# Moving the cross-attention's value products to the front of a streaming-encoder block, and seven more weight pairs by seven products

## The chip, the cores and the metric

The kernel runs on one core of a Trainium2 chip. A core has five engines with queues of their own: TensorE (PE, matmuls; its weight loads are shown as PEld), VectorE (DVE), ScalarE (ACT), GpSimd (POOL, which here issues transfers and a few memsets) and SyncE (SP, which issues most transfers). Operands lie in an on-chip memory of 128 partitions (SBUF); matmuls write to eight banks of a second memory (PSUM), from which VectorE or ScalarE take the results. The metric is the device time of one execution in microseconds; the figure given is the median of several.

## The reference

One layer of an encoder block on 256 positions of width 2048, all in float32, with 256 memory tokens:

```python
x = x + 0.5 * swiglu(rms_norm(x, ffn1_norm), ffn1_w_up, ffn1_w_down)      # d_ff = 5632
h = rms_norm(x, mix_norm);  proj = h @ w_in                              # 10240 columns
...                                  # gated recurrence, convolution with RG-LRU, gated merge
x = x + merged @ w_out
x = x + cross_attention(rms_norm(x, xattn_norm), rms_norm(mem, mem_norm), wq, wkv, wo)
x = x + 0.5 * swiglu(rms_norm(x, ffn2_norm), ffn2_w_up, ffn2_w_down)
return rms_norm(x, final_norm)

def cross_attention(h, m, wq, wkv, wo):                                  # 4 heads of 512
    q = (h @ wq).reshape(B, S, 4, 512)
    k, v = jnp.split(m @ wkv, 2, axis=-1)                                # from mem alone
    p = softmax(einsum('bshd,bmhd->bhsm', q, k) * 512 ** -0.5)
    return einsum('bhsm,bmhd->bshd', p, v).reshape(B, S, D) @ wo
```

The keys and the values depend on the memory tokens and their weights only, not on x.

## The kernel before, in words

**Arithmetic.** Every large product is made from operands split in two parts: a high part, rounded to the format that TensorE multiplies (`h`), and the rest (`l`). A product is then three matmuls: high by high, low by high, high by low (`three`, L905; `rows_product`, L696). ACT writes the high part and DVE subtracts it from the raw weight to get the low one (`split`, L532).

**Weights.** All weights are read from DRAM in pieces of 1 MB, 128 x 2048 numbers each, in a list that is drawn up beforehand (`plan`, L541 on) and followed two pieces ahead (`weights`, L585). A piece is made ready in one of four ways (`prepare`, L636): "plain" is a load and one split of 2048 columns; "added" (`begin_added`, L627) lets ACT write the negative high part and a transfer issued by POOL add the raw weight to it, so that DVE has nothing to do; "fast" adds four sums of weight blocks (two of them in one instruction) and splits 1536 columns of the weight and 2048 of the sums; "made" reads such sums from DRAM, where they were put earlier.

**Feed-forwards.** The up weights of a feed-forward are 11 groups of 8 pairs (g, p). A pair is two row blocks by two column blocks, for two halves of the 256 positions. Eight block products of three matmuls each (24 matmuls of 512 columns) give the plain result; a Strassen-like scheme does it with seven products (21 matmuls) by means of sums of the blocks of x and of the weights (`PRODUCTS`, L917). "mixed" is eight products that add into the same seven PSUM banks as "fast" pairs. Which pair goes which way is in `MIXED` (L43) and `ffn_order` (L50). Before, in the first feed-forward, group 0 is "plain" throughout, groups 1 and 2 have four mixed pairs (0, 2, 4, 6) and four fast ones, the later groups one mixed pair (6, "added") and seven fast ones. The down products (24 matmuls a piece) follow some groups behind. The operands of x are made at the start (`head_x`, L1044; `operand_pairs`, L860): h and l for each pair, the blocks' sums, and the differences that mixed pairs need (`less`).

**The middle.** 176 products of 24 matmuls' time each, with recurrences beside them: input projection, gates, branches, out, then the cross-attention: 16 query products, 16 key products, 16 value products (`wvm`), 16 of `wo`. During the queries the memory tokens are loaded, normalised and split (`ms`, eight of the 24 smaller tiles), and their squares are summed; one fp32 product makes the scale of each token along the columns, and two small ones make it by token. The scores of the four heads (`scores`, L1465) are put among the value products, one step behind each (`pump`). Beside the middle's products POOL loads 56 pieces of the second feed-forward's up weights, DVE makes their sums, and POOL writes these to DRAM (`make_ahead`, L604; `make_sums`, L612): 56 in 154 products.

**Memory.** Tiles of 128 x 2048 ("big": raw, td, h, l, tl, made, own, ev, junk) come from one ring of 9, which has 4 more in the feed-forwards (`FFN_POOLS`, L789). Tiles of 128 x 1024 ("slot") are 24.

**Order.** The program is recorded as operations (`Flow.record`, L211), then put in order by a planner (`arrange`, L291): each operation gets a price (`price`, L254) and a due time, worked back from the matmuls that need it (`aims`, L282), and a list scheduler fills the five queues. It gives out tiles and PSUM banks as they come free by its own prices, and runs twice; the second time with the waits for reused tiles that the first gave. Every queue then runs in that fixed order, so nearly all instructions show the recorder's line, L465.

Of the kernel before, what the change touches and what calls it, by code (L numbers as in the profile page):

```python
# [14 lines left out]
P = 128  # L15
T = 256
# [14 lines left out]
for _name, _n in [  # L31
# [12 lines left out]
    "ffn1": {0: "plain", 1: (0, 2, 4, 6), 3: (6,)},  # L44
    "ffn2": {0: "fast", 1: (), 3: ()},
# [3 lines left out]

def ffn_order(name):  # L50
    mixed = MIXED[name]
    out, down = [(mixed[0], 0, p) for p in range(8)], [("down", 0, 1, c, 0) for c in range(4)]
    for g in range(1, NG):
        if g < 3:
            out += [("mixed" if p in mixed[1] else "fast", g, p) for p in (0, 1, 2, 3, 5, 4, 7, 6)]
        else:
            out += [("mixed" if p in mixed[3] else "fast", g, p) for p in (1, 3, 0, 6, 4, 2, 5, 7)]
# [38 lines left out]
class Buffer(View):  # L96


    def __init__(self, ring, shape, dt, name, room, whole=False):
        grain = shape[1] if whole else 1 if shape[1] <= 128 else 32  # L100
        super().__init__(self, np.arange(shape[1]) // grain)
        self.ring, self.shape, self.dt, self.name, self.room = ring, shape, dt, name, room
# [7 lines left out]
class Ring:  # L110
    def __init__(self, tag, spare):
        self.tag, self.spare = tag, spare
        self.places, self.takers = [], []
# [70 lines left out]
class Flow:  # L184
# [26 lines left out]
    def record(self, queue, method, args, kw):  # L211
# [16 lines left out]
        for v in outs:  # L228
            t = v.tile
            if not t.users:  # L230
                op.takes.append(t)
                t.ring.takers.append(op)
            elif t.users[-1].queue is queue and t.users[-1] is not op:
                op.deps.setdefault(t.users[-1], False)
# [56 lines left out]
    def arrange(self):  # L291
# [178 lines left out]
def block_kernel(tc: tile.TileContext, xT, xin, memT, vec, gfin, bgate, lruw, wu1, wd1, win, wv,  # L470
# [72 lines left out]
    def plan_ffn(name, wu, wd):  # L543
        for e in orders[name]:
            src = wd[e[4], e[3]] if e[0] == "down" else wu[e[1], e[2]]
# [30 lines left out]
    for name, w in (("mv", wvm), ("o", wo)):  # L576
        for g in range(4):
            plan_rows(name, w, g)
    between = between + 2, len(plan) - between - 6
    plan_ffn("ffn2", wu2, wd2)  # L580

    head, rest = [], {}
    planned = count()

    def weights(*key):  # L585
        while plan and len(ahead) < 2:
# [3 lines left out]
            if i < len(head):  # L590
# [13 lines left out]
    def make_ahead(i):  # L604
        n, pieces = len(MADE), between[1] - 16
# [183 lines left out]
    FFN_POOLS = dict(more=4, third=1)  # L789
# [70 lines left out]
    def operand_pairs(name, src, gain, q, xg, out):  # L860
        mixed = MIXED[name]
        both = [p for p in mixed[1] if p not in mixed[3]]

        for a in src:
# [7 lines left out]
            less = None if 2 * q + i not in mixed[1] else (h[:, 512:768], l[:, 512:768])  # L872
            if 2 * q + i in both:
                if 2 * q + i == both[0]:
                    xd.append(slot(F32R, "xd"))
                n = 512 * both.index(2 * q + i)
                less = [xd[-1][:, a:a + 256] for a in (n, n + 256)] if n < 1024 else []
            out.append(((h, l), less))

        def sums(which=((0, "less"), (0, "sums"), (1, "less"), (1, "sums"))):  # L880
            s = slot(name="xs")
            for i, ((h, l), less) in enumerate(out):
# [8 lines left out]
                if less == [] and (i, "less") in which:  # L891
                    third = scoped["third"].tile([P, 512], F32R, name="xd", tag="xd")
                    less.extend((third[:, :256], third[:, 256:]))
                if less and (i, "less") in which:
                    made(*less, 2, 0, lambda o: ((a[0], a[1], ALU.subtract), (a[2], a[3], ALU.subtract)))
                if 2 * q + i not in mixed[3] and (i, "sums") in which:
                    if not i and less and len(which) > 1:
                        s = slot(name="xs")
# [14 lines left out]
    def part(pair, i, n):  # L913
# [7 lines left out]
        "plain": [(0, 0, 1), (1, 0, 2), (0, 1, 0), (1, 1, 3), (2, 2, 1), (3, 2, 2), (2, 3, 0), (3, 3, 3)],  # L921
    }

    def ffn(name, pairs, sq, then, begin=(), sums=(), rstds=()):
# [5 lines left out]
        for e in order:  # L930
            if e[0] != "down":
# [40 lines left out]
        for at, e in enumerate(order):  # L972
# [3 lines left out]
            if kind != "down":  # L976
# [13 lines left out]
                last = at + 1 == len(order) or order[at + 1][1] != g or following == "down"  # L990
                ends = kind != "plain" and uses[g, 0][-1][0] == p
                if ends or last:
                    if ends or kind == "plain":
                        flow.room = room["scope"]
                        ev = big("ev", F32)
                        e0, e1, e2, e3 = (ev[:, i * 512:(i + 1) * 512] for i in range(4))
                        if rstds:
                            rstd = rstds[0]
                        if rstd is None:
                            rstd = sq.rstd_tokens()  # L1000
                if ends:
# [3 lines left out]
                if last:  # L1005
                    if kind == "plain":
                        activate(e0, accs[0], accs[1], 0)
                        activate(e3, accs[3], accs[2], 1)
                    else:
                        for o, n, x in ((e0, 1, e0), (e1, 3, e1), (e1, 2, e1)):  # L1010
                            dve.tensor_tensor(out=o, in0=accs[n], in1=x, op=ALU.add)
                        activate(e0, e0, e1, 0)
                        for o, n, x in ((e3, 6, e2), (e2, 3, e2)):
                            dve.tensor_tensor(out=o, in0=accs[n], in1=x, op=ALU.add)
                        activate(e3, e3, e2, 1)
# [48 lines left out]
    head += [lambda p=p: head_x(p) for p in range(8)]  # L1064
# [6 lines left out]
    for i in range(3):  # L1071
        rest[4 + i] = lambda i=i: head_residual(i)
    for q, i in enumerate((3, 7, 8, 9)):
        rest[i] = lambda q=q: sums1[q](((0, "less"), (1, "sums")))
    made = rest[7], rest[8]
    rest[7] = lambda: [f() for f in (lambda: head_residual(3), made[0])]
    rest[8] = lambda: [f() for f in (head_rstd, made[1])]
    for q, i in ((0, 22), (1, 23), (2, 24)):
        rest[i] = lambda q=q: sums1[q](((0, "sums"),))
# [37 lines left out]
    def to_mix(c, t):  # L1117
# [9 lines left out]
        else:  # L1127
            late2.append(lambda: normed(xs2, c, "mix_norm"))

# [312 lines left out]
    ms, sqm = Operands(), Squares()  # L1442
    for m in range(KT):
# [5 lines left out]
        for i in range(2 * m, 2 * m + 2) if m < 4 else (m + 4,) if m < 12 else ():  # L1449
# [5 lines left out]
            sqm.add(mk)  # L1455
    ks = Operands()
    for m in range(KT):
        acc = product(ms.tiles, weights("k", m))
        if m == 0:
            rmem, rmtok = sqm.rstd(), sqm.rstd_tokens()  # L1460
        ks.add(summed(acc, by=rmem))

    probs = {}
# [31 lines left out]
    side += [scores(h) for h in range(HEADS)]  # L1495
    vs = {}
    for g in range(4):
        accs = [bank(), bank()]
        for kq in range(4):
            rows_product(accs, ms.tiles, weights("mv", g, kq), 4 * kq, kq == 0, kq == 3)  # L1500
            pump(1)
        for t in range(2):
            s = slot(F32R, "vs")
            f = scoped["tmp2"].tile([P, 512], F32, name="vf", tag="part")
            act.activation(f, accs[t], ACT.Copy, scale=rmtok[:, t:t + 1])
# [155 lines left out]
```

## Time and profile before

| | |
|---|---|
| median of 3 runs | 2416.41 us (2416.34 to 2417.48) |
| the profiled execution | 2415.88 us, of it 2414.1 us between first and last instruction |
| PE busy | 2402.7 us, 12130 matmuls |
| DVE busy | 2066.0 us, 2232 instructions |
| ACT busy | 1421.3 us |
| moved by DMA | 662.83 MB, mean 275 GB/s |

The page gives the busy times and forty slices of the span of 60 us each; a digit is a share in tenths. The first feed-forward takes slices 1 to 11 or 12, the middle up to about the 29th, the second feed-forward the rest. The listings give for a group of instructions: engine, operation, what is written and read, the shapes, the count, the busy time, the mean of one in ns, and the idle time of the engine before them. A row of the timeline is start, duration, engine and instruction; a row of the chain is start, duration and what. A row of the table by stretches has the stretch, its length, then busy time and count for PE, PEld, DVE, ACT and POOL, the granted clock of PE, the share of the DMA engines and GB/s. PE's matmuls overlap, so 0.39 us for one is its latency, and the distance of two starts is what it costs.

### The profile page before, as it was taken

Reading aid. Unit: us, or ns where it says so; the run is one execution under the profiler, and the core shown is the slowest. Engines: PE = TensorE matmul, PEld = TensorE weight load, DVE = VectorE, ACT = ScalarE, POOL = GpSimd, SP = SyncE. Lnnn points to the kernel's source line nnn. Section 1 sums busy time; section 2 is a strip of 40 time slices with the busy share of each in tenths; the row PEclk is TensorE's granted clock in tenths of the full one; section 3 lists DMA queues with packets and bytes.
Section 4 is the critical chain, followed back from the end, with each engine's and each line's share of the span. In section 5 each row is a group of like instructions: output and inputs, shape, how many; then the busy total and the mean of one; then the engine's idle time right before and its main releaser. Section 6 shows DMA issues by size and latency. Waiting matters only on the chain.

```text
span 2414.1 us, 30928 instructions
## 1 busy us (share of the span) xinstructions
PE 2402.7 (100%) x12130; PEld 2011.3 (83%) x12130; DVE 2066.0 (86%) x2232; ACT 1421.3 (59%) x1414; POOL 83.2 (3%) x142
## 2 busy tenths in 40 slices
PE   9999999999999999999999999999999999999998
PEld 8888888888888888888888888888888888888887
DVE  8999999999955778788876887767899999999995
ACT  8566666666754443476534654445677666666663
POOL 0000000000000000000000000000000000000000
PEclk9999999999999999999999999999999999999999
DMA  8568787888735688888988988876898677777773
GB/s 317 192 227 261 261 261 244 261 261 258 265 140 192 236 300 296 306 310 313 367 311 315 344 324 325 314 277 253 331 393 316 254 262 261 261 261 261 261 274 114
DMA packets 98354, 662.83 MB, mean 275 GB/s; under 512 B 10912, under 2 KB 11168, under 8 KB 24992
## 3 DMA queue, kind: packets, MB, share of 16 engines
q1 hardware_dynamic: 77904, 517.11, 57.7%
q0 software_dynamic: 19584, 142.62, 18.0%
q8 instruction: 95, 1.56, 0.3%
q10 hardware_dynamic: 720, 1.13, 0.1%
q14 instruction: 51, 0.42, 0.0%
HBM read 574.83 MB, written 60.82 MB: 263 GB/s over the span
## 4 chain that ended last, share of the span: by engine, by line
PE 98%; ACT 1%; DVE 1%; DMA 1%; issue 0%; ACTq 0%; DVEq 0%
PE acc L465 98%; DMA made<-wu 1%; ACT h L465 0%; PE warm L465 0%; DVE l L465 0%; ACT ops L465 0%; DVE made L465 0%; DVE ops L465 0%; ACT junk L465 0%; ACT x L465 0%; DVE ss L465 0%; DVE x L465 0%; DVE gate L465 0%; DVE xc L465 0%; ACTq L465 0%
## 5 line engine op out<-in xcount | busy, mean ns | idle before, releaser
L465 DVE TENSOR_TENSOR l<-raw,h 128x2048 fp32r<-128x2048 f32 (+2 forms) x428 | 870.2, 2037 | 181.4 <-ACT h L465 72.3
L465 ACT ACTIVATE h<-raw 128x2048 fp32r<-128x2048 f32 (+2 forms) x428 | 730.8, 1712 | 401.0 <-PE acc L465 222.8
L465 PE MATMUL acc<-h,xh 128*128 128x512 f32 x1244 | 484.5, 390 | 0.9 <-ACT h L465 0.9
L465 PE MATMUL acc<-h,xl 128*128 128x512 f32 x1244 | 484.0, 389 | 0.0
L465 ACT ACTIVATE h<-td 128x1024 fp32r<-128x1024 f32 (+1 forms) x248 | 307.9, 1250 | 225.4 <-DVE td L465 212.8
L465 PE MATMUL acc<-h,ops 128*128 128x512 f32 x1664 | 398.0, 391 | 0.6 <-DVE gate L465 0.6
L465 DVE TENSOR_TENSOR tl<-td,h 128x1024 fp32r<-128x1024 f32 (+1 forms) x248 | 358.8, 1457 | 16.7 <-ACT h L465 14.8
L465 PEld LDWEIGHTS acc<-h,ops 128*128 128x128 f32 x1664 | 310.0, 188 | 64.8 <-DVE gate L465 1.1
L465 PE MATMUL acc<-h,hidop 128*128 128x512 f32 x1408 | 355.2, 390 | 0.0
L465 PEld LDWEIGHTS acc<-h,hidop 128*128 128x128 f32 x1408 | 262.9, 188 | 53.7
L465 PE MATMUL acc<-ops,h 128*128 128x512 f32 x1152 | 278.3, 393 | 0.3 <-DVE ops L465 0.2
L465 PEld LDWEIGHTS acc<-h,xh 128*128 128x128 f32 x1244 | 233.6, 188 | 51.2 <-ACT h L465 1.5
L465 PEld LDWEIGHTS acc<-h,xl 128*128 128x128 f32 x1244 | 233.6, 188 | 48.1
L465 PEld LDWEIGHTS acc<-ops,h 128*128 128x128 f32 x1152 | 211.6, 188 | 43.3 <-DVE ops L465 1.2
L465 PE MATMUL acc<-l,ops 128*128 128x512 f32 x832 | 206.2, 389 | 0.0
L465 PE MATMUL acc<-l,hidop 128*128 128x512 f32 x704 | 190.3, 389 | 0.0
L465 PEld LDWEIGHTS acc<-l,ops 128*128 128x128 f32 x832 | 155.9, 188 | 32.3
L465 PE MATMUL acc<-l,xh 128*128 128x512 f32 x636 | 175.9, 390 | 0.0
L465 PE MATMUL acc<-tl,xh 128*128 128x512 f32 x608 | 168.2, 390 | 0.0
L465 DVE TENSOR_TENSOR made<-made 128x512 f32<-128x512 f32 x224 | 152.9, 687 | 11.9 <-DMA made<-wu 8.0
L465 PEld LDWEIGHTS acc<-l,hidop 128*128 128x128 f32 x704 | 132.2, 188 | 27.5
L465 PEld LDWEIGHTS acc<-ops,l 128*128 128x128 f32 x1152 | 148.0, 191 | 5.6
(172 smaller groups left out, 1921.9 us busy)
## 6 DMA issues: line engine op xcount, KB each, us to landing
raw<-wu SPq DMA_DIRECT2D x108, 1024.0 KB, 7.0
raw<-wd SPq DMA_DIRECT2D x72, 1024.0 KB, 6.9
made<-wu POOLq DMA_DIRECT2D x56, 1024.0 KB, 6.6
kept<-made POOLq DMA_DIRECT2D x56, 1024.0 KB, 7.1
td<-kept SPq DMA_DIRECT2D x56, 1024.0 KB, 7.2
raw<-wu SPq DMA_DIRECT2D x56, 768.0 KB, 5.6
raw<-win SPq DMA_DIRECT2D x40, 1024.0 KB, 4.8
raw<-wg SPq DMA_DIRECT2D x32, 1024.0 KB, 6.2
```

Of the source, the lines that this page charges most:

```text
L465: getattr(op.queue.real, method)(*map(real, args), **{k: real(v) for k, v in kw.items()})
```

## The change

In the first feed-forward, groups 0, 1 and 2 now have the mixed pairs 0, 4 and 6 (6 as "added") and five fast pairs. The "plain" scheme of a group is gone, and with it a small pool of one tile. The 16 value products of the cross-attention are done in the first feed-forward: three sets of four before group 0, the fourth between groups 0 and 1. The memory tokens are loaded and split for them into four big tiles; they are loaded once more as rows, to be squared with a sum over each row for the scale. Each set's result goes through a small tile to DRAM (512 KB each, issued by POOL) and is read back and split among the key products, beside which the scores of a head now stand. The memory is loaded and split again for the keys, as before. The 56 sums are spread over 140 products of the middle, from 6 products earlier in relation to its start. In its first pass the planner now also knows that a PSUM bank must be read before it is taken again.

```diff
-    "ffn1": {0: "plain", 1: (0, 2, 4, 6), 3: (6,)},
-    "ffn2": {0: "fast", 1: (), 3: ()},
+    "ffn1": ((0, 4, 6), (0, 4, 6), (0, 4, 6)) + ((6,),) * (NG - 3),
+    "ffn2": ((),) * NG,
...
+VALUES = {0: (0, 1, 2), 1: (3,)}
...
+        if name == "ffn1":
+            out += [("mv", i, kq) for i in VALUES.get(g, ()) for kq in range(4)]
+        out += [("mixed" if p in mixed[g] else "fast", g, p)
+                for p in ((0, 4, 1, 2, 6, 3, 5, 7) if g < 3 else (1, 3, 0, 6, 4, 2, 5, 7))]
...
+        if not hasattr(self, "sequence"):
+            for r in {id(t.ring): t.ring for op in ops for t in op.takes if t.whole}.values():
+                for t, op in zip(r.tiles, r.takers[len(r.places):]):
+                    for u in t.users:
+                        if u.i < op.i:
+                            u.after.append(op)
...
-            if e[0] == "mixed" and e[1] > 2:
-                kind = "added"
+            if e[0] == "mixed":
+                kind = "added" if e[1] > 2 or e[2] == 6 else kind
...
-    between = between + 2, len(plan) - between - 6
+    between = between - 4, len(plan) - between
...
-        n, pieces = len(MADE), between[1] - 16
+        n, pieces = len(MADE), between[1] - 20
...
-    FFN_POOLS = dict(more=4, third=1)
+    FFN_POOLS = dict(more=4)
...
+    class BigOperands(Operands):
+        def new(self):
+            i = len(self.tiles) % 4
+            if i == 0:
+                flow.room = room["scope"]
+                self.cur = big("ms")
+            self.tiles.append(self.cur[:, i * 512:(i + 1) * 512])
+            return self.tiles[-1]
...
+    def head_memory(kq):
+        m = slot(name="mem")
+        n = T if kq == 0 else 4 * T
+        for a in range(0, 4 * T, n):
+            sp.dma_start(m[:, a:a + n], memT[:, 4 * kq * T + a:][:, :n])
+            for j in range(a, a + n, T):
+                ms1.add(m[:, j:j + T], col("mem_norm", 4 * kq + j // T))
+
+    def head_squares():
+        ss = small.tile([P, 2 + PAD], F32, name="ssm", tag="ssm", bufs=1)[:, :2]
+        for t in range(2):
+            m = big("memory", F32)
+            sp.dma_start(m, mem[t])
+            act.activation(m, m, ACT.Square, accum_out=ss[:, t:t + 1])
+        act.activation(ss, ss, ACT.Sqrt, bias=eps, scale=1.0 / D)
+        dve.reciprocal(out=rmtok, in_=ss)
+
+    head.update({kq: lambda kq=kq: head_memory(kq) for kq in range(4)})
...
+    def memory_values(g, kq, w):
+        if kq == 0:
+            values[g] = [bank(), bank()]
+        accs = values[g]
+        rows_product(accs, ms1.tiles, w, 4 * kq, kq == 0, kq == 3)
+        if kq == 3:
+            f = slot(name="values")
+            for t in range(2):
+                act.activation(f[:, t * 512:(t + 1) * 512], accs[t], ACT.Copy, scale=rmtok[:, t:t + 1])
+            values[g] = dram.tile([P, 1024], F32, name=f"values{g}", tag=f"values{g}")
+            gps.dma_start(values[g], f)
...
-    ms, sqm = Operands(), Squares()
+    ms = Operands()
...
+    def take_values(g):
+        f = slot(name="values")
+        sp.dma_start(f, values[g])
         for t in range(2):
             s = slot(F32R, "vs")
+            r = f[:, t * 512:(t + 1) * 512]
+            split(s[:, :512], s[:, 512:], r)
             vs[g, t] = s
+
+    for m in range(KT):
+        acc = product(ms.tiles, weights("k", m))
+        if m == 0:
+            rmem = by_feature(rmtok)
+        ks.add(summed(acc, by=rmem))
+        if m % 4 == 3:
+            side.append(scores(m // 4))
+            take_values(m // 4)
+        pump(1)
     pump(1 << 30)
```

More of the change, by code (lines that the diff above doesn't have):

```diff
@@ L467, in emit, with block_kernel @@
                 inner.close()
-def block_kernel(tc: tile.TileContext, xT, xin, memT, vec, gfin, bgate, lruw, wu1, wd1, win, wv,
+def block_kernel(tc: tile.TileContext, xT, xin, memT, mem, vec, gfin, bgate, lruw, wu1, wd1, win, wv,
                  wg, wab, wout, wq, wk, wvm, wo, wu2, wd2, out_):
@@ L889, in made @@
                     split(h, l, s[:, at:at + n * P])
[L891 to L898, printed above, removed]
+                if less:
+                    made(*less, 2, 512 * i, lambda o: ((a[0], a[1], ALU.subtract), (a[2], a[3], ALU.subtract)))
+                if 2 * q + i in both:
+                    s = slot(name="xs")
+                if 2 * q + i not in mixed[-1]:
                     made(h[:, 512:], l[:, 512:], 4, 512 * i,
@@ L1454, in block_kernel @@
             ms.add(mk, col("mem_norm", i))
[L1455 to L1463, printed above, removed]
+    probs, ks, vs = {}, Operands(), {}
     def scores(h):
```

122 lines of the change are left out of this document (54 added, 68 removed).

## The prediction

> **What bounds the kernel now.** I read the page first: the busy times, then the slices.
>
> ```profile
> span 2414.1 us, 30928 instructions
> PE 2402.7 (100%) x12130; PEld 2011.3 (83%) x12130; DVE 2066.0 (86%) x2232; ACT 1421.3 (59%) x1414; POOL 83.2 (3%) x142
> PE   9999999999999999999999999999999999999998
> DVE  8999999999955778788876887767899999999995
> DMA  8568787888735688888988988876898677777773
> ```
>
> TensorE is busy throughout, VectorE is nearly full in the two feed-forwards (the first eleven and the last nine slices) and has room in the middle. Since a busy PE isn't yet a PE at its rate, the next views were the chain of waits and the timeline of PE.
>
> ```profile
> 7.13 104.75 PE acc L465 x470
> 111.89 583.11 PE acc L465 x2618
> ```
>
> ```profile
> 304.41 0.39 PE L465 MATMUL acc<-h,xh 128*128 128x512 f32 x1
> 309.17 0.39 PE L465 MATMUL acc<-h,xh 128*128 128x512 f32 x1
> ```
>
> The chain is one string of products. The two PE rows are the first matmuls of two consecutive seven-product pairs: 21 matmuls in 4.76 us, 0.2267 us each, which is also the commonest step between neighbours everywhere else. So a saved matmul is worth 0.2267 us, and there are hardly any holes to win. The waits of PE's weight loads confirm that: the one on VectorE's last split is the third longest, six times and 1.4 us in all.
>
> ```profile
> PEld acc L465 <- ACT h L465: 1.5, 2, 1.1
> PEld acc L465 <- DVE tl L465: 1.4, 6, 0.4
> PEld acc L465 <- DVE gate L465: 1.1, 1, 1.1
> ```
>
> The shapes in the listing by form give VectorE's prices, and one of ACT's (count, then busy us and mean ns):
>
> ```profile
> L465 DVE TENSOR_TENSOR l<-raw,h 128x2048 fp32r<-128x2048 f32 x260 | 593.8, 2287 | 168.9 <-ACT h L465 66.4 <-PE acc L465 53.7 <-issue 26.4
> L465 DVE TENSOR_TENSOR l<-raw,h 128x1536 fp32r<-128x1536 f32 x152 | 266.0, 1751 | 12.0 <-ACT h L465 5.6 <-PE acc L465 5.3 <-DMA l<-own 0.3
> L465 DVE TENSOR_TENSOR tl<-td,h 128x1024 fp32r<-128x1024 f32 x192 | 232.5, 1216 | 14.7 <-ACT h L465 13.3 <-PE acc L465 1.1
> L465 DVE TENSOR_TENSOR td<-raw,td 128x512 f32<-128x512 f32 x192 | 131.0, 682 | 0.4
> L465 DVE TENSOR_TENSOR td<-raw 128x1024 f32<-128x1024 f32 x96 | 116.7, 1216 | 0.7 <-PE acc L465 0.7
> L465 DVE TENSOR_TENSOR ev<-acc,ev 128x512 f32<-128x512 f32 x147 | 97.6, 685 | 12.5 <-PE acc L465 9.5 <-ACT ev L465 1.2
> L465 DVE SCALAR_TENSOR_TENSOR ev<-ev,rtok 128x512 f32<-128x512 f32 x42 | 31.3, 745 | 0.0
> L465 DVE TENSOR_TENSOR hidop<-acc,hidop 128x512 fp32r<-128x512 f32 x44 | 28.7, 681 | 0.7 <-ACT hidop L465 0.7
> L465 DVE TENSOR_TENSOR xl<-xg,xh 128x512 fp32r<-128x512 f32 x16 | 10.8, 683 | 0.4 <-ACT xh L465 0.4
> L465 DVE TENSOR_TENSOR xs<-xg 128x128 f32<-128x128 f32 x38 | 10.6, 284 | 4.5 <-ACT xg L465 4.2
> L465 ACT ACTIVATE ops<-mem,vt 128x256 fp32r<-128x256 f32 x16 | 7.0, 501 | 0.0
> L465 DVE SCALAR_TENSOR_TENSOR ops<-mem,vt,ops 128x256 fp32r<-128x256 f32 x16 | 7.0, 478 | 0.0
> ```
>
> A pair by seven products costs VectorE 1.216 + 2 x 0.682 + 1.751 + 2 x 1.216 = 6.76 us against 4.76 us of PE; a pair by eight costs 2.29 us against 24 x 0.2267 = 5.44, and one of kind "added" nothing. That is why not every pair goes by seven.
>
> **The change, part by part.** *Seven pairs.* Group 0 goes from none by seven to five, groups 1 and 2 from four to five each: seven pairs, 3 matmuls each, 21 x 0.2267 = 4.76 us less PE. This is on the path.
>
> *The values' products.* Their 16 x 24 matmuls (87.1 us of PE) move from the cross-attention to the front, at no change for PE. Their splits move along (16 x 2.29 = 36.6 us of VectorE), so each four of them bring 21.8 us of PE for 9.2 of VectorE.
>
> *Is VectorE enough at the front?* Group 0 with its twelve value products: twelve splits 27.4, pairs 0 and 4 4.6, five by seven 33.8, pair 6 nothing, sixteen memory operands 7.6, low parts of x 5.5, sums of x 7 x (4 x 0.284 + 0.683) + 3 x about 1 = 15.7, eviction 7 x 0.685 + 2 x 0.745 = 6.3, turned hidden 1.4: 102 us. PE there: 15 x 5.44 + 5 x 4.76 = 105.4. That is 97%. The old group 1 ran at the same share:
>
> ```profile
> 56.78:109.35 52.57, 52.57 (x239) 43.62 (x238) 50.42 (x48) 29.47 (x26) 0.00 (x0) 1.00 0.56 200
> 300.00:362.00 62.00, 62.00 (x279) 51.21 (x278) 58.82 (x61) 42.42 (x36) 2.61 (x3) 1.00 0.79 254
> ```
>
> 50.42 of 52.57 us are 96%, without a hole in PE, and later groups hold four pairs by seven in a row at 95%. Group 1 gets easier (four value products more), group 2 is near 100%, with 13 large tiles as now.
>
> *The large tiles.* Here lies the risk. The normalised memory takes four of the 13 until the last value product in group 1, so group 0's pairs work with nine. A pair by seven holds h, l, th, tl (four) while PE multiplies it, and the next needs up to five while it is made. Both fit, but nothing is left to load a third.
>
> ```profile
> raw<-wu SPq DMA_DIRECT2D x108, 1024.0 KB, 7.0
> l<-own POOLq DMA_DIRECT2D x24, 1024.0 KB, 8.1
> raw<-win SPq DMA_DIRECT2D x40, 1024.0 KB, 4.8
> ```
>
> The order is 0 4 1 2 6 3 5 7. Say pair 3's weights can be loaded only when PE ends pair 1. They land 7.0 us later; VectorE then needs 3 x 6.76 = 20.3 us for pairs 3, 5, 7 and is done at 27.3; the last four matmuls (0.9 us) come behind, 28.2. PE alone would be through at 4.76 + 5.44 + 3 x 4.76 = 24.5. So the upper end is a stall of 3.7 us. The lower end is 0, if the load goes out one tile earlier. I take 0.5, nearest to the 0.4 us that the longest such wait lasts now. Pair 6 also needs POOL's adding transfer (8.1 us, behind a copy on ACT); POOL's queue has nothing else there but the values' writes, and l is read only after 16 of the pair's matmuls.
>
> By the Trainium skill's page DMA: Bandwidth & Descriptors, Anatomy of one DMA, a transfer takes about 2.0 us plus its bytes at 436 GB/s, an estimate of 4.4 us for 1 MB. The stall above would then be 1.1 us and not 3.7, the mild rival below 2411.9 and not 2414.5; the rows (4.8 at the quickest, 7.0 here) put it between, and the sum goes by them.
>
> *The start.* The first matmul waits for ACT:
>
> ```profile
> 4.63 2.50 PE L465 MATMUL warm<-ones 128*128 128x128 f32 x16
> 4.28 0.91 ACT L465 ACTIVATE xg<-xf,vt 128x256 f32<-128x256 f32 x2 [1.61 <-DMA vt<-vec]
> 5.22 0.63 ACT L465 ACTIVATE xh<-xg 128x512 fp32r<-128x512 f32 x1
> 6.89 0.48 PE L465 MATMUL acc<-h,xh 128*128 128x512 f32 x1
> ```
>
> Now it needs one gained copy (0.50, the ACT row of mem above) and a weight piece, not two copies, xh and a piece: about 1.1 us less ACT ahead of it. The last sixteen warm-up records begin from 4.63 at about 0.11 us apart, so PE is free from about 6.3; the gain is 0 to 0.6, and I take 0.5. SP must issue eight loads, not five, for that product, which could take it back.
>
> *Traffic at the front.* Twelve weights, both forms of mem, xT and xin in twelve products of 5.44 us: 12 x 1.05 + 4 x 2.1 = 21 MB in 65 us, 323 GB/s. It was already higher there:
>
> ```profile
> 30.00:35.00 5.00, 5.00 (x24) 4.14 (x23) 4.96 (x9) 4.97 (x10) 0.00 (x0) 1.00 1.05 424
> 1020.00:1030.00 10.00, 10.00 (x48) 8.42 (x47) 8.88 (x15) 6.92 (x8) 0.54 (x1) 1.00 1.01 418
> 1100.00:1200.00 100.00, 100.00 (x447) 83.07 (x446) 82.54 (x86) 57.20 (x63) 6.97 (x13) 1.00 0.93 349
> ```
>
> Cost 0.
>
> *The middle.* The 56 sums for the second feed-forward now spread over 140 products, not 154. Each product moves 1.05 MB and 2.1 x 56/140 = 0.84 MB, against 0.76: 4.2% more, 364 GB/s where there were 349. The transfers reached 418 in the same stage, so I price it at 0.1: the one wait of 1.1 us on DVE gate, quoted above, where VectorE's queue stood behind a sum whose load landed late, made 10% likelier by 10% denser sums. The upper bound is in the rivals.
>
> *The memory's scale.* One matmul over 256 columns stays (on another tile). The four one-column matmuls go:
>
> ```profile
> L465 PE MATMUL acc<-ones,ss x4: 167/250/250, 1448.2 to 1448.5; 128*128 128x1 f32 x4
> ```
>
> About 0.45 us with the turn between kinds. Squares of the memory (16 on ACT, 15 adds on DVE) leave the query stage, two large squares enter the front: no engine there is the bound; 0.
>
> *The tail of the scores.* The last head's scores no longer lie under value products. After the last key product: copy, sum, scale, split, about 3 us; two sets of score products 2.8; softmax to ps:
>
> ```profile
> 1552.47 0.42 DVE L465 TENSOR_TENSOR p<-acc,lo 128x256 f32<-128x256 f32 x1
> 1555.88 0.57 ACT L465 ACTIVATE ps<-acc 128x512 fp32r<-128x512 f32 x1
> 1632.51 11.45 PE L465 MATMUL acc<-ps,vs 128*128 128x512 f32 x64
> ```
>
> 3.4 us from the first of these rows to the second, 1.3 for ps: near 11 us in all. Three of four heads' output products (11.3 x 3/4 = 8.5 us) and, after them, three products of wo (16.3 us) need none of it. Bounds 0 and 2.5; I take 0, as the planner lets a ready matmul pass a waiting one. The values' reads come with the key products, behind one weight each on SP.
>
> *The sum*, against the profiled execution of 2415.88 us (span 2414.1, 1.8 around it; the median of the runs is 0.5 above): -4.76 - 0.45 - 0.5 + 0.5 + 0.1 = -5.1, 2410.8, on the median's footing 2411.3. Two runs of this kernel differ by under 0.05%, and I call 0.2%, 4.8 us, the least that tells it from no change; the forecast is just beyond.
>
> **The rivals.** *Group 0 short of tiles, mildly*: the 3.7 us come about. For it: nine tiles, 97% of VectorE. Against: the middle stage runs on nine, though with plain products. 2411.3 + 3.2 = 2414.5, no change.
>
> *Group 0 starved* (slower). If a pair's weights can be loaded only once the preceding pair is fully made, each costs 7.0 + 6.76 = 13.8 us against 4.76, 9 us a pair. One such pair gives 2420, within 0.2%; from two on it is slower, 2429. For it: of nine tiles, squares' scraps, ev and pair 6's own and l take some too. Against: ordinary pairs release h after 6 of 21 matmuls. The order comes from a planner that deals out tiles by its own estimate of durations.
>
> *The tail is exposed*: if wo's products can't pass, 2.5 us (2414); if the heads' outputs can't either, 11 us, 2422.
>
> *The transfers' limit.* If no more than about 350 GB/s came through for long (the 349 above were at a share of 0.93), the middle's 4.2% would lengthen some 100 us by 4: 2415.3. The trace's 418 and 424 speak against it. The Trainium skill has such a rule (DMA: Bandwidth & Descriptors, Where 436 GB/s comes from): about 358 GB/s from HBM for a core binds; the rows above exceed it.
>
> *A new order throughout*: the planner's first pass now knows of PSUM's reuse, which moves due times in every stage. Today's order has few holes, so there is more to lose than to gain: two or three holes of the size of the tail above, 10 us, would give 2421.
>
> **How the numbers follow.** Forecast (2409.5 to 2411.6) 0.42; mild shortage 0.20; starved 0.22; tail 0.06, of it 0.04 slower; limit 0.05; new order 0.05, slower. Faster 0.42, same 0.20 + 0.02 + 0.05 = 0.27, slower 0.22 + 0.04 + 0.05 = 0.31 (the two last lie at the bound or over it). The range, 2409 to 2426, takes in the start's best bound, the mild cases and half of the starved ones.
>
> **What would show it.** PE should have 21 matmuls fewer of 512 columns in the first feed-forward and four of one column fewer; the front's chain should stay one string of products, its DVE row at 9. A wait of PE or its loads on ACT h, DVE l or tl between about 70 and 115 us shows the shortage, and SP waiting there on PE or on DVE tl says it is tiles. A hole behind the last key product (near 1540 us) shows the tail; waits on made loads or a share near 1.0 between 1100 and 1400 show the transfers. The prediction fails if PE's string breaks in group 0 for over 5 us.

## The result, and the profile after

| | before | after |
|---|---|---|
| median | 2416.94 us (2416.33 to 2418.08) | 2431.69 us (2431.25 to 2432.91) |
| ratio | | 1.0061, interval 1.0048 to 1.0074 |
| span of the profiled execution | 2414.1 us | 2429.9 us |

The changed kernel is 14.8 us slower; a gain of 5.1 us was forecast, and the range ended at 2426. The page of the changed kernel, the lines that answer to those shown of before (busy times, then digits by slice):

```profile
span 2429.9 us, 31006 instructions
PE 2419.3 (100%) x12105; PEld 2005.8 (83%) x12105; DVE 2090.5 (86%) x2270; ACT 1442.8 (59%) x1432; POOL 88.6 (4%) x149
PE   9999999999999999999999999999999999999998
DVE  7899999999996677888787878887789999999994
DMA  9675877777774578798898898887798667667773
```

PE has 25 matmuls fewer, as the change says, and is busy 16.6 us longer. It has no more holes than before: 10.6 us of the span lie outside its busy time, against 11.4. The chain is still one string of products, and the longest waits of the weight loads (total, times, longest) are no rival to 15 us:

```profile
PEld acc L478 <- DVE tl L478: 3.9, 9, 0.7
PEld acc L478 <- ACT h L478: 1.8, 6, 0.6
```

So the products themselves must be slower. Two rows of the page's costliest groups of the changed kernel say where: the down products of the feed-forwards (`h` by `hidop`) and products of the middle (`h` by `ops`), both 1408 of the same shape (count, then busy us, mean ns):

```profile
L478 PE MATMUL acc<-h,hidop 128*128 128x512 f32 x1408 | 360.7, 394 | 0.0
L478 PE MATMUL acc<-h,ops 128*128 128x512 f32 x1408 | 336.9, 391 | 0.0
```

In the kernel before, the down products took 5.5 us less:

```profile
L465 PE MATMUL acc<-h,hidop 128*128 128x512 f32 x1408 | 355.2, 390 | 0.0
```

The middle's 336.9 will not move in the run that repairs the kernel (e5 below), while the 360.7 falls to 355.8. How much is lost is seen by counting matmuls in a stretch of a feed-forward. The table by stretches, for the kernel before:

```profile
2000.00:2300.00 300.00, 300.00 (x1346) 248.92 (x1345) 292.78 (x253) 185.32 (x144) 0.00 (x0) 1.00 0.71 264
300.00:600.00 300.00, 300.00 (x1345) 248.40 (x1344) 283.31 (x290) 205.22 (x167) 13.03 (x15) 1.00 0.79 254
```

and for the changed kernel:

```profile
2000.00:2300.00 300.00, 300.00 (x1325) 245.11 (x1324) 288.54 (x248) 184.86 (x143) 0.00 (x0) 1.00 0.70 257
300.00:600.00 300.00, 300.00 (x1325) 244.99 (x1323) 280.55 (x284) 202.32 (x166) 12.12 (x14) 1.00 0.78 254
```

PE reads 300.00 busy of 300 us in all four rows, at a granted clock of 1.00, and yet does 1325 matmuls where it did 1346 (40 of them of 128 columns in either kernel). The 21 missing ones, 1.6%, are worth 4.7 us in 300, and the feed-forwards last about 1360 us: some 21 us, against which the change saves 5. PE never stands idle in these rows and the other engines' busy times fall, so none of the others sets the pace. The Trainium skill says (Trainium Kernel Development and Optimization, Performance Expectations) that the busy share of the weight loads shows better how near TensorE is to its limit than that of the matmuls, as the matmuls are pipelined. These rows agree: the loads' busy time falls from 248.92 to 245.11 us where the matmuls' stands still.

It is not each product that is slower. The timeline of PE in the changed kernel, one seven-product pair into the next (start, duration):

```profile
2099.18 0.40 PE L478 MATMUL acc<-h,xh 128*128 128x512 f32 x1
2099.42 0.40 PE L478 MATMUL acc<-h,xl 128*128 128x512 f32 x1
...
2101.29 0.39 PE L478 MATMUL acc<-h,xl 128*128 128x512 f32 x1
2101.52 0.86 PE L478 MATMUL acc<-l,xh 128*128 128x512 f32 x3
2102.22 1.08 PE L478 MATMUL acc<-tl,xh 128*128 128x512 f32 x4
2103.13 0.39 PE L478 MATMUL acc<-h,xh 128*128 128x512 f32 x1
...
2103.81 0.39 PE L478 MATMUL acc<-h,xl 128*128 128x512 f32 x1
```

From 2099.18 to 2101.52 are ten steps of 0.234 us, from 2101.52 to 2103.13 seven steps of 0.230, and behind these three of 0.227. The kernel before does eight in 1.82 us, 0.2275 each, with none of the slow kind:

```profile
2099.33 1.98 PE L465 MATMUL acc<-h,hidop 128*128 128x512 f32 x8
2101.15 1.07 PE L465 MATMUL acc<-l,hidop 128*128 128x512 f32 x4
```

**What tells slow from quick products.** The instructions are the same; what can differ is where their operands lie. The changed kernel adds two tiles so small that the prediction doesn't count them: the memory's scale by token `rmtok` (8 bytes per partition, next to the constants) and its sums of squares `ssm` (72 bytes, among the small tiles). Each takes up a multiple of 32 bytes, and each moves all that is allotted behind it: `rmtok` moves everything by 32, `ssm` moves by 96 what comes after the small tiles, which is the ring's four further tiles for the feed-forwards (`FFN_POOLS`, "further" below). The addresses in the built programs, in bytes within a partition:

```
kernel    first of nine  first slot  first further  further - nine  mod 256
before          20096       93824       192640         172544          0
after           20128       93856       192768         172640         96
```

Raw weights and sums, the moving operands, lie in the nine or in the further tiles; the stationary ones (`xh`, `xl`, `hidop`, `ops`) lie in slots, 288 x 256 bytes behind the nine in both kernels. In the rows above, the ten slow steps read `h` from two of the further tiles (at 205056 and from 192768 to 198912, each 96 mod 256 away from its stationary operand); the `l`, the `tl` and the `h` from 2103.13 on lie in the nine (44704 to 91808, at 0). That is a correlation; the experiments move addresses and nothing else.

### The profile page after: what moved, and what is told of

Same layout as the page of the kernel before. It is cut to its first block, busy times and chain, and to the rows that moved or that the text cites. A ratio compares the mean times of both kernels' runs of the same rounds, so it can differ in the third digit from the quotient of the medians.

```text
span 2429.9 us, 31006 instructions
## 1 busy us (share of the span) xinstructions
PE 2419.3 (100%) x12105; PEld 2005.8 (83%) x12105; DVE 2090.5 (86%) x2270; ACT 1442.8 (59%) x1432; POOL 88.6 (4%) x149
## 5 line engine op out<-in xcount | busy, mean ns | idle before, releaser
L478 DVE TENSOR_TENSOR l<-raw,h 128x2048 fp32r<-128x2048 f32 (+2 forms) x425 | 860.1, 2028 | 173.9 <-ACT h L478 80.3
L478 ACT ACTIVATE h<-raw 128x2048 fp32r<-128x2048 f32 (+2 forms) x425 | 722.1, 1705 | 383.5 <-PE acc L478 176.2
L478 PE MATMUL acc<-h,xl 128*128 128x512 f32 x1237 | 475.5, 392 | 0.0
L478 ACT ACTIVATE h<-td 128x1024 fp32r<-128x1024 f32 (+1 forms) x262 | 322.9, 1241 | 227.9 <-DVE td L478 171.7
L478 DVE TENSOR_TENSOR tl<-td,h 128x1024 fp32r<-128x1024 f32 (+1 forms) x262 | 375.6, 1448 | 8.6 <-PE acc L478 5.2
L478 PE MATMUL acc<-h,hidop 128*128 128x512 f32 x1408 | 360.7, 394 | 0.0
L478 PE MATMUL acc<-h,ops 128*128 128x512 f32 x1408 | 336.9, 391 | 0.0
L478 PEld LDWEIGHTS acc<-h,ops 128*128 128x128 f32 x1408 | 262.7, 188 | 54.0
L478 PEld LDWEIGHTS acc<-h,xl 128*128 128x128 f32 x1237 | 232.4, 188 | 51.6
L478 PE MATMUL acc<-tl,xh 128*128 128x512 f32 x636 | 177.4, 395 | 0.6 <-DVE tl L478 0.6
L478 PE MATMUL acc<-l,ops 128*128 128x512 f32 x704 | 174.3, 389 | 0.0
L478 PEld LDWEIGHTS acc<-l,ops 128*128 128x128 f32 x704 | 132.1, 188 | 27.4
```

Source lines behind the costliest of these rows:

```text
L478: getattr(op.queue.real, method)(*map(real, args), **{k: real(v) for k, v in kw.items()})
```

## The experiments

Theories: **A**, the addresses: products run slower where moving and stationary operands are not at a common distance modulo some number of bytes. **B**, what the prediction feared: group 0 short of tiles, VectorE, or the denser transfers. **C**, the new order throughout. Medians are compared with the kernel before as timed beside them (2416.40 for e1 to e4, 2416.06 for e5 to e8, 2415.94 for e9 to e12, 2416.94 for the result above). Only e11 and e12 change how a weight pair is multiplied; no run leaves work out.

**First, all to whole multiples.** e1 pads both small tiles, e2 only one:

```diff
-    ms1, rmtok = BigOperands(), const.tile([P, 2], F32, name="rmtok")
+    ms1, rmtok = BigOperands(), const.tile([P, 16], F32, name="rmtok")[:, :2]     # e1 only
-        ss = small.tile([P, 2 + PAD], F32, name="ssm", tag="ssm", bufs=1)[:, :2]
+        ss = small.tile([P, 32], F32, name="ssm", tag="ssm", bufs=1)[:, :2]       # e1 and e2
```

> The changed kernel with two small tiles made larger (rmtok 64 bytes a partition instead of 8, the squares' sums 128 instead of 72), nothing else; all big tiles and slots then begin at a multiple of 64 bytes, as in the kernel before. Theory A (addresses): in the changed kernel the products of both feed-forwards follow each other 230.4 ns apart instead of 226.9 because the nine big tiles and the slots begin at 32 modulo 64 while the four further big tiles begin at 0; with all at 0 the spacing is 226.9 again, 21 us go, and the kernel takes about 2410.5, faster than before by 6. Theory B (the prediction's rival: group 0 is starved of tiles): the padding changes nothing, 2431.7. Theory C (PE is slowed by the greater load of the other engines on the memory): nothing changes either, 2431.7.

> The changed kernel with the squares' sums' tile at 128 bytes only: all thirteen big tiles and the slots then begin at 32 modulo 64. Theory A in the form that only a mixture of the two offsets slows a product: 226.9 ns in the feed-forwards, about 2410.5. Theory A in the form that 32 modulo 64 costs by itself too (products of two operands at 32 follow each other 228.5 to 228.9 ns apart in the changed kernel's feed-forwards): the mixed ones gain 5.3 ns each, 1900 of them, 10 us, about 2421.5. Theories B and C: 2431.7.

Measured: 2426.6 (ratio 1.0041, 1.0028 to 1.0053) and 2426.29 (1.0040, 1.0027 to 1.0052). A gain of 5 us out of 15, and the same for both; none of the times forecast for the two came. A multiple of 64 is not what counts, but addresses do something: a third of the loss went with 56 bytes of padding. In both kernels the further tiles are 172672 behind the nine, 128 mod 256.

**Second, the old kernel with the new addresses.** The order and the work stay the old ones:

```diff
+    gps.memset(small.tile([P, 8], F32, name="pad", tag="pad", bufs=1), 0.0)       # e3 only
-    par = const.tile([P, 96], F32, name="par")
+    par = const.tile([P, 104], F32, name="par")                                   # e3 and e4
```

> The kernel before with 32 bytes more in one constant tile and a 32 byte tile more among the small ones (one memset on GpSimd), so that its big tiles and slots lie as in the changed kernel: nine and the slots at 32 modulo 64, four at 0; order of all other instructions as before. Theory A: the feed-forwards' products at 230.4 ns, about 5830 of them by 3.6 ns, 21 us more, about 2437.5. Theories B and C: 2416.9, as before.

> The kernel before with 32 bytes more in one constant tile: all big tiles and slots at 32 modulo 64. Only a mixture slows: 2416.9. 32 by itself costs too, about 1.8 ns for each of some 5830 products: about 2427. Theories B and C: 2416.9.

Measured: e3 2434.01 (1.0071, 1.0058 to 1.0083), 17.6 us slower than before by 64 bytes of unused memory (and a memset of 32 of them); e4, where everything moves by 32 together, 2415.94 (0.9997, 0.9988 to 1.0006), no difference. The same stretch as above, in e3:

```profile
2000.00:2300.00 300.00, 300.00 (x1327) 245.49 (x1326) 289.05 (x248) 183.52 (x143) 0.00 (x0) 1.00 0.69 257
```

and in e4:

```profile
2000.00:2300.00 300.00, 300.00 (x1346) 248.93 (x1345) 292.76 (x253) 185.15 (x144) 0.00 (x0) 1.00 0.72 264
```

The old kernel falls to the changed one's pace by layout alone (x1327), and keeps its own where all is moved alike (x1346). B and C are not needed for the loss.

**Third, the modulus.** The changed kernel with the further tiles at a distance of 172800 (0 mod 256, not mod 512) and 173056 (0 mod 1024), and the old kernel at 172672 (128):

```diff
-        ss = small.tile([P, 2 + PAD], F32, name="ssm", tag="ssm", bufs=1)[:, :2]
+        ss = small.tile([P, 64], F32, name="ssm", tag="ssm", bufs=1)[:, :2]       # e5; 128 in e6
```

```diff
+    gps.memset(small.tile([P, 32], F32, name="pad", tag="pad", bufs=1), 0.0)      # e7, kernel before
```

> The changed kernel with the squares' sums' tile at 256 bytes a partition instead of 72: the four further big tiles then begin a multiple of 256 bytes behind the nine and the slots (172800 bytes behind the first big tile; 172544 before, 172640 in the changed kernel, 172672 in the first two experiments). Theory A2 (what counts is the distance of the two operands of a product modulo 256 bytes, since the kernel before with everything moved by 32 was as fast as before, and with 128 between the two sorts of tiles a product takes 232.4 ns): 226.9 ns throughout the feed-forwards, 2410.5 or 6 us faster than before. If the modulus is 512 or more, some 229 ns remain and 2420 to 2426. Theory B2 (another cause in the changed kernel, such as the denser work of the other engines, holds the 10 us left over in the first two experiments): 2426.

> The same with 512 bytes: distance 173056, a multiple of 1024. Theory A2: as the run with 256, 2410.5. If the modulus is 512: 2410.5 here and more there. Theory B2: 2426 in both.

> The kernel before with a small tile of 128 bytes more, so that its four further big tiles begin 128 modulo 256 behind the others. Theory A2: the feed-forwards' 5830 products at about 229.4 ns instead of 226.9, 14 us more, 2431. Theory B2 (the 10 us belong to the changed kernel alone): 2417.

Measured: e5 2415.05 (0.9993, 0.9984 to 1.0002), e6 2415.18 (0.9997, 0.9988 to 1.0006), e7 2429.60 (1.0056, 1.0044 to 1.0069). With 184 more bytes for one small tile the changed kernel goes from 14.8 us over the kernel before to 1.0 under it, so some 16 us come back; a common distance modulo 256 is enough, modulo 128 isn't. The 2410.5 forecast for e5 and e6 is missed by 4.6 (the fourth part comes to that). The stretch in e5, and its down products from the page's groups:

```profile
2000.00:2300.00 300.00, 300.00 (x1345) 249.03 (x1344) 292.80 (x253) 185.29 (x144) 0.00 (x0) 1.00 0.71 264
```

```profile
L478 PE MATMUL acc<-h,hidop 128*128 128x512 f32 x1408 | 355.8, 391 | 0.0
L478 PE MATMUL acc<-h,ops 128*128 128x512 f32 x1408 | 336.9, 391 | 0.0
```

The traces with the addresses beside them, as the mean distance in ns from the start of a 128x512 product of the feed-forwards to that of the next, sorted by (moving - stationary address) mod 256. Distances of 300 ns and more are left out as holes:

```
kernels                    distance 0       other distance
before, e4, e5, e6        226.9 to 227.0    (none)
e1, e2, e7                228.1             128: 232.3 to 232.4
e3                        228.6              32: 233.4
after                     228.7              96: 234.1
```

A third of these products use a further tile. In the middle, which has only the nine, the mean is 227.5 to 227.6 in all these kernels.

Two more readings of the same traces narrow it. The value products of the changed kernel have either operand in a further tile: with both there the distance is 0 and a product takes 227.6 ns in e1 (229.9 in the changed kernel); with the stationary one alone there it takes 232.5 in e1 and 233.9 in the changed kernel (distance 160), as slow as with the moving one alone. So it is the pair of places that counts, and not the further tiles. And in the kernels that mix distances, the products at 0 are held up only just behind the others: the first ten after a product at another distance take 229.2 to 230.4 ns on the mean, those from the eleventh on 226.8 to 226.9 (changed kernel, e1, e2, e3, e7).

**Fourth, what is left once the addresses are right.** e5 gains 1.0 us on the kernel before (its interval includes no change), not 5.1. e8 is e5 with all four sets of value products ahead of group 0; e9 is e5 with `rmtok` padded too, as in e1 (nine, slots and further tiles all at a multiple of 64); e10 has both:

```diff
-VALUES = {0: (0, 1, 2), 1: (3,)}
+VALUES = {0: (0, 1, 2, 3)}                                                        # e8, e10, e12
```

> The run with 256 bytes, with the fourth set of value products before group 0 too: the memory's four big tiles are free before group 0's pairs, which then have all 13, while nothing lies between group 0 and group 1. If group 0 is short of tiles, as the prediction feared (0.5 to 3.7 us), this gives that back, less what the eviction of group 0 costs without products behind it; if not, it is the same or slower than the run with 256 bytes by up to 3 us.

> The changed kernel with rmtok at 64 bytes and the squares' sums at 256: all big tiles and slots at a multiple of 64 and the two sorts of big tiles a multiple of 256 apart, as in the kernel before. If only the distance modulo 256 counts: as the run with 256 bytes alone, 2415.0 within 1. If tiles at 32 modulo 64 also make transfers later (adding transfers of 14 us near 391 us there, 10 in the changed kernel), the holes at 418 and 430 us go and it takes about 2413.

> The same with all sixteen value products before group 0. If its gain of 2.3 us in the earlier form belongs to the order, 2.3 us under the run beside it; if it came from the holes at 418 and 430 us, which are a matter of when transfers land, the difference is under 1 us here.

Measured: e8 2412.72 (0.9986, 0.9977 to 0.9995), e9 2414.37 (0.9993, 0.9985 to 1.0002), e10 2412.45 (0.9984, 0.9975 to 0.9992). A common shift by 32 costs at most the 0.2 to 0.6 us by which e10 gains more than e8 and e9 more than e5, near what the runs can tell. The fourth set ahead of group 0 gains 1.9 to 2.3, and not for the reason that was expected of e8: group 0 has no hole worth the name in e5 (next section). The stretches that show where, in e5:

```profile
250.00:300.00 50.00, 49.29 (x217) 39.55 (x217) 49.13 (x50) 35.81 (x31) 2.61 (x3) 1.00 0.88 274
195.00:250.00 55.00, 54.99 (x247) 45.03 (x245) 53.20 (x56) 33.17 (x28) 0.86 (x1) 1.00 0.62 207
400.00:432.00 32.00, 31.07 (x139) 24.92 (x138) 27.21 (x31) 20.42 (x18) 1.73 (x2) 1.00 0.85 261
```

and in e10:

```profile
250.00:300.00 50.00, 50.00 (x223) 40.65 (x223) 49.19 (x51) 35.64 (x30) 1.72 (x2) 1.00 0.78 251
195.00:250.00 55.00, 54.75 (x245) 44.67 (x244) 54.97 (x57) 33.96 (x30) 0.86 (x1) 1.00 0.67 228
400.00:432.00 32.00, 32.00 (x147) 26.57 (x146) 28.50 (x31) 22.05 (x19) 1.73 (x2) 1.00 0.86 272
```

In both, VectorE is full from 250 to 300 us, in group 2. From 195 to 300 us PE does 464 matmuls in e5 and 468 in e10; the four are worth 0.9 us. In e10 VectorE did 1.8 us more beforehand (54.97 of 55 us); why the order lets it is not shown. The larger part lies from 400 to 432 us, eight matmuls or 1.8 us; that hole is traced in the next section. It is still there in e9 (from 380 to 432 us PE lacks 0.97 us, as e5 lacks 0.93), so it does not come of the shift by 32.

e11 and e12 give pairs back to eight products: e11 one in each of groups 1 and 2 on top of e9, e12 one in group 2 on top of e10.

```diff
-    "ffn1": ((0, 4, 6), (0, 4, 6), (0, 4, 6)) + ((6,),) * (NG - 3),
+    "ffn1": ((0, 4, 6), (0, 2, 4, 6), (0, 2, 4, 6)) + ((6,),) * (NG - 3),        # e11
+    "ffn1": ((0, 4, 6), (0, 4, 6), (0, 2, 4, 6)) + ((6,),) * (NG - 3),           # e12
```

> The run with 64 and 256 bytes, with pair 2 of groups 1 and 2 by eight products again, so five more pairs by seven and not seven. By the price of a pair alone (0.68 us) 1.4 us slower. If group 2 lacks VectorE (97 to 98% busy from 195 to 300 us, with 1.8 us of holes in PE between 245 and 280 us), those holes go and it is as fast or faster by up to 0.5 us.

> All sixteen value products before group 0, and pair 2 by eight products again in group 2 alone, where VectorE is fullest: 0.7 us more work for PE against up to 1.5 us of holes. If group 2's holes are VectorE's, 0 to 0.8 us faster than the run with the values first; if not, 0.7 slower.

Measured: e11 2414.91 (0.9997, 0.9988 to 1.0006), 0.5 over e9; e12 2411.86 (0.9981, 0.9973 to 0.9990), 0.6 under e10. The six matmuls of e11 are 1.36 us, so by the medians two pairs by seven are worth 0.5, and 0.9 went into holes. In e12 a pair by eight is no worse than by seven. The intervals of e9 and e11 overlap, and so do those of e10 and e12, so no more is claimed. Its group 2:

```profile
250.00:300.00 50.00, 50.00 (x225) 41.06 (x225) 49.12 (x51) 36.55 (x30) 2.60 (x3) 1.00 0.87 269
```

e12 beats both kernels: it lies 4.1 us under the one before, which itself lies 14.8 under the changed one.

Not tried: the new work without the planner's new rule, since it has no order for it then; so C has no run of its own.

## Why the prediction was wrong

**The step that failed** is "21 matmuls in 4.76 us, 0.2267 us each, which is also the commonest step between neighbours everywhere else. So a saved matmul is worth 0.2267 us". It was measured on the old layout and taken for a property of the matmul; it holds for the products that are left out only if the others keep their pace. In the changed kernel they took 228.7 and 234.1 ns in the feed-forwards instead of 226.9, and that cost some 16 us. With it went "*The memory's scale* ... no engine there is the bound; 0": two tiles were priced by the engines that write them, not by what they move in memory. No rival held this, and so the range ended at 2426.

Where the time went, by the starts of the matmuls of the profiled executions (steps over the nominal distance in the kernel before are "holes", slower products included):

```
                              after - before    e5 - before    e10 - before
first product starts               -0.74           +0.71           +0.31
25 matmuls fewer                   -5.25           -5.25           -5.25
holes, first feed-forward         +11.55           +3.97           +0.76
holes, middle                      +0.38           -0.46           -0.94
holes, second feed-forward        +10.17           +1.18           +1.24
last product starts               +16.11           +0.15           -3.88
```

So the addresses take 7.6 us in the first feed-forward and 9.0 in the second (after less e5), and with them right, 4.7 of the 5.25 us are still lost to small holes (e5). Some of these holes come only with the right addresses, it seems because slow products had given VectorE time. e5's weight loads wait more often than the changed kernel's:

```profile
PEld acc L478 <- DVE tl L478: 4.9, 12, 0.7
PEld acc L478 <- ACT h L478: 3.5, 11, 0.6
```

Point by point:

- *Seven pairs, and the one-column matmuls*: right, 12130 to 12105 and 5.25 us by the nominal distances (4.76 + 0.45 forecast).
- *The values' products are no change for PE*: right by the same count.
- *VectorE at the front, 97%*: too high. In the changed kernel it was busy for 85.94 of the 105 us from 7 to 112, and the pairs of group 0 ran at the same 82%:

```profile
66.00:113.00 47.00, 47.00 (x205) 38.23 (x205) 38.59 (x38) 34.80 (x36) 2.62 (x4) 1.00 0.69 237
```

- *Traffic at the front, 323 GB/s*: more came, 372, as here in e5 from 7 to 66 us. The cost of 0 was right all the same, PE is full:

```profile
7.00:66.00 59.00, 59.00 (x264) 48.99 (x264) 47.89 (x86) 51.45 (x87) 0.00 (x0) 1.00 0.99 372
```

- *The large tiles, 0.5 with bounds 0 and 3.7; starved at 0.22*: wrong in weight. The sign named for it came, SyncE waiting for a tile (from 60 to 113 us in the changed kernel):

```profile
SPq L478 <- DVE tl L478: 18.0, 1, 18.0
```

  PE has no hole there for all that (47.00 of 47). In e5, where slow products can't hide one, the same stretch lacks 0.03 us:

```profile
66.00:113.00 47.00, 46.97 (x208) 38.59 (x207) 39.06 (x38) 34.99 (x36) 2.62 (x4) 1.00 0.69 239
```

- *Group 2 is near 100%*: the share was right (49.13 of 50 us in e5), and the conclusion that it costs nothing was not: of the first feed-forward's 4.0 us of added holes about half lie between 245 and 280 us, and some 0.8 of them go when the values come first (e10). Another 1.8 lie between 400 and 432 us, and all of them go in e10. They begin with an adding transfer of POOL, issued at 391.53 us in e5. It lands 14.1 us later; the one that answers to it in e10 takes 10.3 (transfers issued from 388 to 406 us, e5 and then e10):

```profile
l<-own POOLq DMA_DIRECT2D x1, 1024.0 KB, 14.1
l<-own POOLq DMA_DIRECT2D x1, 1024.0 KB, 10.3
```

  Until it has landed it holds its tile (`own`, at 201120 in e5), and the next high part is to be written there. So ACT waits for it, VectorE for ACT, and VectorE then works without a pause up to 419.9 us. The split that begins at 417.02 gives the low part for which PE's weight loads wait, 1.0 us at once (rows of ACT and VectorE, then the waits of the weight loads from 416 to 420 us, all of e5):

```profile
405.75 1.92 ACT L478 ACTIVATE h<-raw 128x2048 fp32r<-128x2048 f32 x1 [1.76 <-DMA l<-own]
407.70 2.29 DVE L478 TENSOR_TENSOR l<-raw,h 128x2048 fp32r<-128x2048 f32 x1 [1.09 <-ACT h L478]
417.02 2.28 DVE L478 TENSOR_TENSOR l<-raw,h 128x2048 fp32r<-128x2048 f32 x1
```

```profile
PEld acc L478 <- DVE l L478: 1.0, 1, 1.0
```

  In e10 neither ACT nor VectorE waits at that place. So tiles did run short for a moment, in a group that the prediction didn't consider, and by a transfer that it priced at 8.1 us. What made this one slow is not shown.
- *The start, -0.5*: -0.7 in the changed kernel, +0.7 in e5 and +0.3 in e10, and the rows were misread. The warm-up matmuls in the kernel before begin 0.21 us apart up to 5.70 us and 0.11 apart only from 5.85 on. The last begins at 6.86, not at 6.3, and the first product 0.03 behind it: PE was at its warm-up, it did not wait for ACT. So it is in the profiled executions of the changed kernel, e5 and e10 too. In e5 the memory's copy is ready at 5.22 us, and the first product begins at 7.60, behind the last warm-up at 7.57:

```profile
4.73 0.49 ACT L478 ACTIVATE ms<-mem,vt 128x256 fp32r<-128x256 f32 x1
4.63 3.21 PE L478 MATMUL warm<-ones 128*128 128x128 f32 x16
7.60 1.63 PE L478 MATMUL acc<-h,ms 128*128 128x512 f32 x6
```

  The last warm-up matmul at the slow pace begins at 4.20 us in the changed kernel, at 5.70 before, at 6.34 in e10 and at 7.19 in e5, and this makes the differences. What sets that moment is not shown; a scatter of this size was in no bound.
- *The middle, +0.1, and the transfers' limit*: the middle got 0.5 to 0.9 shorter where the addresses were right. The changed kernel moved up to 372 GB/s over a whole slice of 60 us in it (the 24th), with PE's digit at 9. The Trainium skill (DMA: Bandwidth & Descriptors, Where 436 GB/s comes from) names about 358 as the limit of a core; this slice exceeds it, as the prediction's rows did:

```profile
GB/s 364 242 274 180 260 259 255 249 258 248 254 256 177 182 290 325 268 349 330 328 339 329 327 372 337 331 312 260 291 372 299 255 247 264 257 258 259 260 273 113
```

- *The tail of the scores, 0 with bounds 0 and 2.5*: right. The last key product ends near 1636 us in the changed kernel, not near 1540. PE has no hole behind it, and the first products of `wo` (from 1646.63) do pass the last head's output products (from 1651.46):

```profile
1600.00:1700.00 100.00, 100.00 (x519) 85.23 (x518) 80.10 (x133) 56.91 (x97) 5.95 (x11) 1.00 0.77 279
```

- *A new order throughout*: not tried alone. e5 has that order and isn't slower than before; what the order can have cost by itself is the 1.2 us of the second feed-forward, whose work is the same.

With the addresses right, the rival that comes nearest is the forecast's own sum less the holes: 0.9 to 1.6 us of gain (e5, e6, e9) for 5.1, and 3.5 (e10) with the values first.

## What to carry to other kernels

Before you price what a change adds, see what it moves: a tile of 72 bytes displaced the pool behind it and cost three times what the change was to gain, with the busy shares of TensorE, VectorE and ScalarE unchanged. Count matmuls per stretch, or measure from start to start, since the busy share of the matmuls does not show a slower product. In a kernel like this one, pad small pools so that all large pools start at the same address modulo 256, and where two kernels differ by per cents with no wait between them, compare addresses before theories.

## What the runs showed of the hardware

TensorE's pace for 128x512 products depended on where the moving operand lay in relation to the stationary one, modulo 256 bytes: 226.9 to 227.0 ns at 0, 232.3 to 232.4 at 128, 233.4 at 32, 234.1 at 96, and 233.9 at 160 (value products). In a kernel that mixes distances the products at 0 took 228.1 to 228.7, all of it within ten products of one at another distance. The absolute address did not count: the further tiles were quick at 160 and 192 mod 256 (e5, e12) where the nine lay at the same, and slow at 192 (e3) where the nine lay at 160. Nor is it a change from one moving tile to the next: the ten slow steps shown lie in tiles a multiple of 2048 bytes apart. The runs don't show what in the chip does this. As the next product's stationary operand nearly always lies at the same distance as the product's own, they don't show which of the two counts either. Other distances have no runs (224 stands in eight products of e3 alone).

The other surprise is how far it reaches: 64 unused bytes made a tuned kernel 17.6 us slower (e3).
